# Even and odd outputs from channel sums: a new channel transform in the Fourier layer of a two-layer encoder

## The chip, the cores and the metric

The kernel runs on one core of one Trainium2 chip. The core has five engines, each with its own instruction queue that is worked off in order: PE (matmuls and transposes), DVE, ACT, POOL, and SP, which here only starts transfers. The metric is the device time of one execution in microseconds, the median of several runs; lower is better. One execution was also recorded by the hardware profiler, and all rows shown come from that recording.

## The reference

An encoder trunk of two layers runs on a prompt of 2048 positions and a sample of 512, with 1024 channels. Layer 0 is windowed attention. Layer 1, where the change lies, is a Fourier layer:

```python
def fourier_layer(x, g, w_gate, w_out):
    b, s, d = x.shape
    h = rmsnorm(x, g)
    hg = h.astype(jnp.float32).reshape(b, s, N_FGROUPS, FGROUP_CH)     # 4 groups of 256 channels
    f = jnp.fft.fftn(hg, axes=(1, 3), norm="ortho").real
    f = f.reshape(b, s, d).astype(x.dtype)
    gate = h @ w_gate
    return x + (f * jax.nn.silu(gate)) @ w_out
```

A final RMSNorm follows. The transform over a group's 256 channels is a product with a fixed 256x256 table of cosines and sines; the transform over positions comes later, out of its results.

## The kernel before

**Numbers.** [...] `matmul3` forms a product as higher x higher, higher x lower and lower x higher: three matmuls.

**The stage that matters.** The 20 tiles of 128 positions are worked off as ten `Pair`s. `gates(pr, hooks)` forms the gate of one pair as a two-by-two Strassen product in the order of its accumulators W, Z and X: W with B11, Z with T1 (on S1), W with T2 (on S2), Z with B22 (on S4), W with T3 (on S3), W with N4, and four short pieces of X between them; each is 12 matmuls of 512 columns, X is four times 3. Between these products the hooks prepare the next pair, `nx`:

- `norms` normalises its two tiles x[1] and x[0]; `turn` transposes one 512-channel half on PE into a PSUM bank and makes both parts of it (tile `tT`, ACT and DVE);
- `sums` forms F1, F2, F3 and F4, sums and differences of the transposed halves of the two tiles, in the tiles `s1` and `s4`; `parts` makes the two parts of each (tiles `S1` to `S4`, ACT and DVE);
- `z` is the channel transform: 24 matmuls of 256 columns for a tile, 12 for each of its halves `z..._0` and `z..._1`, on the parts of the transposes and the table `chan_sb`; ACT copies each half out of PSUM;
- `silu` turns a finished quarter of the gate (`c`, `c12` or W) into a tile `gt` (ACT tanh, DVE product), and POOL starts its store;
- after every second pair `combine` does a radix-4 step over the four z tiles of a group (six DVE additions of 1024 columns).

**What sets the order.** A scheduler puts the instructions into the five queues from the order of the text, the dependences and the free buffers; afterwards each queue is fixed. Buffers come from pools by tag. Two tags matter here: `x`, with four buffers of which one holds `chan_sb` throughout the stage, so that the tiles x[1], x[0], `c`, `s1` and `s4` of successive pairs share three; and `bank`, five PSUM banks for the transposes and z.

The buffers of the tag `x` are handed on like this before: `s1` of the next pair takes the buffer of that pair's x[1], which is free once its eight transposes have run.

The names of tiles carry numbers: `trb12_0` is a transpose of tile 12, `S1_3` the parts of F1 of pair 3, which is made of the tiles 12 and 8 and prepared inside the gates of pair 2 (`W2`, `X2`, `c2`).

Of the kernel before, what the change touches and what calls it, by code (L numbers as in the profile page):

```python
# [19 lines left out]
P = 128  # L20
# [11 lines left out]
HALVES = ((1, 0), (1, 1), (0, 0), (0, 1))  # L32
# [11 lines left out]
def encoder(  # L44
# [97 lines left out]
    def attention_phase():  # L142

        with ExitStack() as es:
# [484 lines left out]
            def gate_sums(k):  # L629
# [3 lines left out]
                def load():  # L633
                    for r in (k, k + 4):
# [69 lines left out]
            def quarters(place, k):  # L704

                t = ready["B", k] = place([P, 2, 512], F32, f"w32B_{k}")
                for half, r in enumerate((k, k + 4)):
                    after(SP.dma_start(t[:, half], w_gate[half, r // 2, :, (r % 2) * 512 : (r % 2) * 512 + 512]), last_exp[0])

            def ahead():  # L710

                def transform():
                    t = ready["chan"] = xtile([P, 2, 2, 256], F32R, "chan_sb")
                    after(POOL.dma_start(t, chan), last_exp[0])
# [17 lines left out]
                steps = dict(zip((42, 45, 48, 52), quarter + [transform]))  # L732
# [128 lines left out]
    def fourier_phase(tail):  # L861
        with ExitStack() as es:
# [55 lines left out]

            class Pair:
                def __init__(self, n, ts):  # L920
                    self.n, self.ts, self.x, self.ps, self.A, self.F, self.S = n, ts, [None, None], {}, {}, {}, {}
                    self.zs = [None, None]
# [11 lines left out]
                def turn(self, i, hf):  # L934
# [3 lines left out]
                    for k in range(4):  # L938
                        c0 = (hf * 4 + k) * P
                        PE.transpose(ps[:, k * P : (k + 1) * P], self.x[i][:, c0 : c0 + P], ident)  # L940
                    t = main.tile([P, 2, 512], F32R, align_bytes=LINE, tag="hT", bufs=8, name=f"tT{name}")
                    ACT.copy(t[:, 0], ps)
                    DVE.tensor_tensor(t[:, 1], ps, f32(t[:, 0]), ALU.subtract)
                    self.ps[i, hf], self.A[i, hf] = ps, (t[:, 0], t[:, 1])
# [16 lines left out]
                def parts(self, i):  # L961
                    self.S[i] = split(left([P, 2, 512], F32R, f"S{i}_{self.n}"), self.F[i])

                def z(self, i, hf):

                    t = self.ts[i]
                    if hf == 0:
                        self.zs[i] = zt(f"z{t}")
                    ps = bank(f"z{t}_{hf}")
                    a = self.A[i, hf]  # L970
                    for gg in range(2):
                        for kk in range(2):
                            ks = slice((gg * 2 + kk) * P, (gg * 2 + kk + 1) * P)
# [129 lines left out]
            def turns1(pr):  # L1103
                pr.turn(1, 0)
                pr.turn(1, 1)
                pr.sums(1)

            def turns2(pr):
# [5 lines left out]
                pr.parts(2)  # L1114

# [28 lines left out]
            for i, hf in HALVES:  # L1144
                pr.z(i, hf)
            for k in range(4):
                build(k)
            for n, pr in enumerate(pairs[:-1]):
                nx = pairs[n + 1]
                for i in range(2):  # L1150
# [4 lines left out]
                    5: [lambda: nx.z(1, 0), lambda: nx.z(1, 1)],  # L1155
                    6: [lambda: nx.z(0, 0), lambda: nx.z(0, 1), lambda: combine(nx)],
# [504 lines left out]
```

## Time and profile before

| | |
|---|---|
| median of three runs | 1620.09 us (1619.69 to 1620.53) |
| the profiled execution: its time / its span | 1622.4 us / 1620.6 us |
| busy: PE, DVE, ACT, POOL | 99%, 69%, 54%, 27% of the span |
| granted PE clock, mean | 0.995 |
| Fourier stage with z (first to last z matmul) | 1084.8 to 1330.9 us |
| one pair, from one W with B11 to the next | 26.63 us (1144.59 to 1171.22) |

The span is what the profiler saw between the first and the last instruction; the time has some start and end around it. A row of the timeline gives the start, the length of a run of like instructions, the engine, the line and the operation, and in brackets how long the engine had been idle and what ended that. A row of the groups gives the busy time and the mean length of one instruction in ns. PE's ends are modelled: consecutive matmuls overlap, so the step from one to the next is read from the starts of two rows, not from their lengths.

### The profile page before, as it was taken

How to read it: one execution, taken by the hardware profiler on the slowest of the kernel's cores; microseconds unless marked ns; L12 is line 12 of the kernel's file. 1: busy time of each engine (PE TensorE's matmuls, PEld its weight loads, DVE VectorE, ACT ScalarE, POOL GpSimd, SP SyncE). 2: the span in 40 equal slices, each digit the busy share in tenths (PEclk: the TensorE clock that was granted, in tenths of full speed). 3: DMA queues.
4: the chain of work that ended last, by engine and by line, in shares of the span. 5: the costliest groups of instructions: out<-in, count | busy, mean ns of one | idle time of the engine just before them, and what ended most of it. 6: DMA issues, size and time to landing. Idle time of an engine off the chain costs nothing.

```text
span 1620.6 us, 27520 instructions
## 1 busy us (share of the span) xinstructions
PE 1598.9 (99%) x9835; PEld 1334.6 (82%) x9835; DVE 1116.6 (69%) x2799; ACT 870.2 (54%) x2043; POOL 431.1 (27%) x605
## 2 busy tenths in 40 slices
PE   9999999999999999999999999999999999999998
PEld 7777888888888888978788888888888887888886
DVE  6788665777547776367754577668576767988696
ACT  6687644676237674157752476546545554343252
POOL 2456551421403414024222242211112111100010
PEclk9999999999999999999999999999999999999999
DMA  7487696656765567655659566666456469455952
GB/s 300 157 314 272 227 351 218 227 215 211 287 220 197 214 237 259 225 205 214 242 166 326 203 219 228 236 217 248 170 208 241 172 220 407 153 195 195 348 201 91
DMA packets 100644, 374.16 MB, mean 231 GB/s; under 512 B 12139, under 2 KB 22379, under 8 KB 83100
## 3 DMA queue, kind: packets, MB, share of 16 engines
q1 hardware_dynamic: 81708, 297.91, 51.8%
q0 software_dynamic: 16464, 70.30, 11.1%
q10 hardware_dynamic: 2336, 4.20, 0.7%
q8 instruction: 78, 1.28, 0.3%
q14 instruction: 58, 0.48, 0.1%
HBM read 281.10 MB, written 91.26 MB: 230 GB/s over the span
## 4 chain that ended last, share of the span: by engine, by line
PE 87%; DMA 5%; DVE 4%; ACT 2%; issue 1%; POOL 1%; SPq 0%; POOLq 0%; DVEq 0%; ACTq 0%
PE qp L95 13%; PE gp L95 12%; PE op L95 8%; PE spt L95 8%; PE W L95 6%; PE spt L441 6%; PE av L525 6%; PE fo L95 5%; PE z L95 4%; PE vp L95 4%; PE Z L95 3%; PE pt L499 3%; PE Wo L95 2%; PE X L95 2%; PE trb L940 1%; DMA xs<-in_x_dram 1%
## 5 line engine op out<-in xcount | busy, mean ns | idle before, releaser
L95 PE MATMUL qp<-h,wq 128*128 128x512 f32 x960 | 239.9, 399 | 0.2 <-DVE pts L508 0.2
L95 PE MATMUL gp<-h,wg 128*128 128x512 f32 x960 | 237.7, 396 | 0.0
L460 DVE CUSTOM_DVE_ANT_0 S<-spt,b 128x385 f32<-128x385 f32 (+1 forms) x320 | 156.9, 527 | 115.6 <-PE spt L441 115.2
L507 ACT CAST pts<-pt 128x384 fp32r<-128x384 f32 (+1 forms) x320 | 123.8, 472 | 185.6 <-PE pt L499 185.4
L95 PEld LDWEIGHTS qp<-h,wq 128*128 128x128 f32 x960 | 176.6, 190 | 42.6 <-issue 5.2
L95 PEld LDWEIGHTS gp<-h,wg 128*128 128x128 f32 x960 | 175.2, 188 | 43.5 <-issue 9.7
L468 ACT ACTIVATE S<-S 128x385 f32<-128x385 f32 (+1 forms) x320 | 190.1, 605 | 35.6 <-DVE S L460 35.1
L508 DVE TENSOR_TENSOR pts<-pt,pts 128x384 fp32r<-128x384 f32 (+1 forms) x320 | 147.3, 522 | 25.7 <-ACT pts L507 24.7
L549 POOL TENSOR_TENSOR uT<-o,uT 128x256 fp32r<-128x256 f32 x75 | 55.5, 740 | 358.9 <-ACT uT L548 358.9
L95 PE MATMUL op<-wo,uT 128*128 128x512 f32 x600 | 140.4, 391 | 0.0
L95 PE MATMUL fo<-wo,tTu 128*128 128x512 f32 x576 | 140.3, 395 | 0.0
L441 PE MATMUL spt<-kwin,qab 64*128 64x384 f32 (+1 forms) x960 | 132.6, 358 | 5.7 <-DVE S L460 5.6
L95 PEld LDWEIGHTS op<-wo,uT 128*128 128x128 f32 x600 | 111.9, 188 | 23.9 <-issue 0.7
L95 PEld LDWEIGHTS fo<-wo,tTu 128*128 128x128 f32 x576 | 106.8, 190 | 20.5
L525 PEld LDWEIGHTS av<-pts,v 128*128 128x128 f32 x576 | 101.4, 188 | 19.0 <-DVE pts L508 0.4
L441 PEld LDWEIGHTS spt<-kwin,qab 64*128 64x128 f32 x960 | 85.1, 185 | 37.5 <-issue 27.5
L525 PE MATMUL av<-pts,v 128*128 128x512 f32 (+1 forms) x576 | 115.9, 341 | 0.0
L95 PE MATMUL spt<-wo,uT 128*128 128x512 f32 x360 | 86.7, 392 | 0.0
L480 DVE TENSOR_SCALAR S<-S 128x384 f32<-128x384 f32 (+1 forms) x192 | 79.2, 413 | 5.3
L543 DVE TENSOR_TENSOR o<-av,t 64x256 f32<-64x256 f32 x150 | 62.6, 417 | 26.4 <-ACT t L534 25.0
L95 PEld LDWEIGHTS spt<-wo,uT 128*128 128x128 f32 x360 | 66.5, 188 | 13.7
L499 PEld LDWEIGHTS pt<-ident,S 64*128 64x128 f32 x1792 | 68.8, 138 | 6.2 <-issue 2.3
(304 smaller groups left out, 2937.5 us busy)
## 6 DMA issues: line engine op xcount, KB each, us to landing
wo<-wsd SPq DMA_DIRECT2D x32, 1024.0 KB, 5.2
wq<-wsd SPq DMA_DIRECT2D x31, 1024.0 KB, 7.4
wg<-wsd SPq DMA_DIRECT2D x31, 1024.0 KB, 4.9
x<-x1d SPq DMA_DIRECT2D x40, 512.0 KB, 3.6
b<-b21d SPq DMA_DIRECT2D x40, 512.0 KB, 5.1
b<-rowd SPq DMA_DIRECT2D x40, 384.0 KB, 4.3
xs<-in_x_dram SPq DMA_DIRECT2D x23, 512.0 KB, 6.5
s2d<-gt POOLq DMA_DIRECT2D x40, 256.0 KB, 3.4
```

The source lines that it names most:

```text
L95: pe(PE.matmul(out, a[i], b[j], start=start and i + j == 0, stop=stop and i == 1, skip_group_check=more))
L441: pe(PE.matmul(banks[j][:, 2 + k0 * P : 2 + k1 * P], res["q"][rows, qp, b * P : (b + 1) * P], kwin[g][rows, kp, b * P + k0 * P : b * P + k ...
L460: seq(DVE, DVE.tensor_tensor_reduce(out=s[:, e0:e1], in0=ps[:, 1 + e0 : 1 + e1], in1=st["bias"][:, j, 386 - e1 : 386 - e0][:, ::-1], scale ...
L468: last_exp[0] = seq(ACT, ACT.activation(s[:, e0:e1], s[:, e0:e1], AF.Exp, bias=s[:, 386:387], scale=-1.0, accum_out=s[:, 387:388]))
L480: seq(DVE, DVE.tensor_scalar(s[:, ks], s[:, ks], den, None, ALU.mult))
L499: pe(PE.transpose(ps[h][:, kb, j, :], ss[j][rows, 1 + kb * P : 1 + (kb + 1) * P], ident[rows, rows]))
L507: seq(ACT, ACT.copy(hi, ps[:, k0:k1]))
L508: seq(DVE, DVE.tensor_tensor(lo, ps[:, k0:k1], f32(hi), ALU.subtract))
L525: pe(PE.matmul(to, v, pt, start=n == part == 0, stop=part == 1 and n in (1, len(todo) - 1), skip_group_check=n > 1,))
L543: seq(DVE, DVE.tensor_tensor(o[64 * j : 64 * j + 64], ps[0:64, :, j], t2[:, :, j], ALU.add))
L549: low = eng.tensor_tensor(lo, o, f32(hi), ALU.subtract)
L940: PE.transpose(ps[:, k * P : (k + 1) * P], self.x[i][:, c0 : c0 + P], ident)
```

## The change

The channel transform is split by the parity of the output. For one group, the even outputs are a product of the sum of its two channel halves with a 128x128 table, the odd ones of the difference. `turn` therefore transposes, for each hf, the four groups' halves hf instead of four neighbouring blocks, and the gate's weights are paired to match (rows 2k and 2k+1 in place of k and k+4). What z multiplies is now:

- tile x[1]: even from F1 (which the gate's Strassen sums have anyway, `S1`), odd from the new `mb`, F1 minus twice the second half;
- tile x[0]: even from the new `ma`, odd from a new `mb`.

`mix` forms these f32 sums in place, in the x tiles themselves. `low` makes the parts: the higher one by ACT, the lower one by POOL in two pieces of 256 columns. It serves `ma`, `mb` and, in place of DVE, all four `parts`. The table's 256 columns hold its higher and its lower part side by side; so z takes 4 matmuls of 256 columns for a group (16 for a tile, 24 before), in a PSUM bank of its own, and the two 128-column results of each product are added on the way out: ACT copies one, DVE adds the other, into every second column. The transform's tile of `turn(1, 0)` is no longer made. The table is loaded raw into a free attention tile, and four ACT copies sort it.

```diff
             def ahead():
                 def transform():
+                    t = ready["table"] = ap.tile([P, 640], F32, tag="invb", name="chan32")[:, :512]
+                    after(POOL.dma_start(t, chan[:, 0].rearrange("p a c -> p (a c)")), last_exp[0])
+                def even_odd():
                     t = ready["chan"] = xtile([P, 2, 2, 256], F32R, "chan_sb")
-                    after(POOL.dma_start(t, chan), last_exp[0])
+                    src = ready["table"].rearrange("p (a n o) -> p o a n", a=2, o=2)
+                    for low in range(2):
+                        for odd in range(2):
+                            dst = t[:, low, odd].rearrange("p (a n) -> p a n", a=2)
+                            seq(ACT, ACT.activation(dst, src[:, odd], AF.Copy, scale=0.5 if low else 1.0))
...
                     for k in range(4):
-                        c0 = (hf * 4 + k) * P
+                        c0 = (k * 2 + hf) * P
                         PE.transpose(ps[:, k * P : (k + 1) * P], self.x[i][:, c0 : c0 + P], ident)
-                    t = main.tile([P, 2, 512], F32R, align_bytes=LINE, tag="hT", bufs=8, name=f"tT{name}")
-                    ACT.copy(t[:, 0], ps)
-                    DVE.tensor_tensor(t[:, 1], ps, f32(t[:, 0]), ALU.subtract)
-                    self.ps[i, hf], self.A[i, hf] = ps, (t[:, 0], t[:, 1])
+                    self.ps[i, hf] = ps
+                    if (i, hf) != (1, 0):
+                        t = htile([P, 2, 512], F32R, f"tT{name}")
+                        ACT.copy(t[:, 0], ps)
+                        DVE.tensor_tensor(t[:, 1], ps, f32(t[:, 0]), ALU.subtract)
+                        self.A[i, hf] = t[:, 0], t[:, 1]
+                def low(self, t, src):
+                    ACT.copy(t[:, 0], src)
+                    for j in range(2):
+                        cs = slice(j * 256, j * 256 + 256)
+                        POOL.tensor_tensor(t[:, 1, cs], src[:, cs], f32(t[:, 0, cs]), ALU.subtract)
+                    return t[:, 0], t[:, 1]
+                def mix(self, i):
+                    x, t = self.x[i].rearrange("p (o n) -> p o n", o=2), self.ts[i]
+                    if i == 0:
+                        ACT.copy(x[:, 0], self.ps[0, 0])
+                        DVE.tensor_tensor(x[:, 0], x[:, 0], self.ps[0, 1], ALU.add)
+                        self.M[0, 0] = self.low(htile([P, 2, 512], F32R, f"ma{t}"), x[:, 0])
+                    both = x[:, 0] if i == 0 else self.F[1]
+                    DVE.scalar_tensor_tensor(x[:, 1], self.ps[i, 1], -2.0, both, ALU.mult, ALU.add)
+                    self.M[i, 1] = self.low(htile([P, 2, 512], F32R, f"mb{t}"), x[:, 1])
...
                 def parts(self, i):
-                    self.S[i] = split(left([P, 2, 512], F32R, f"S{i}_{self.n}"), self.F[i])
-                def z(self, i, hf):
+                    self.S[i] = self.low(left([P, 2, 512], F32R, f"S{i}_{self.n}"), self.F[i])
+                    if i == 1:
+                        self.M[1, 0] = self.S[1]
+                def z(self, i):
                     t = self.ts[i]
-                    ...
-                            matmul3(
-                                ps[:, gg * 256 : gg * 256 + 256], (a[0][:, ks], a[1][:, ks]),
-                                (ch[:, kk, 0], ch[:, kk, 1]), kk == 0, kk == 1,
-                            )
-                    ACT.activation(
-                        self.zs[i][:, hf * 512 : hf * 512 + 512], ps, AF.Copy, scale=1.0 if t >= SEQ // P else 0.5
-                    )
+                    self.zs[i] = zt(f"z{t}")
+                    for g in range(4):
+                        ps = bank(f"z{t}_{g}")
+                        gs = slice(g * P, (g + 1) * P)
+                        for odd in range(2):
+                            m = self.M[i, odd]
+                            for part in range(2):
+                                PE.matmul(
+                                    ps[:, odd * 256 : odd * 256 + 256], m[part][:, gs], ch[:, t < SEQ // P, odd],
+                                    start=part == 0, stop=part == 1,
+                                )
+                        v = ps.rearrange("p (o a n) -> p a o n", o=2, a=2)
+                        out = self.zs[i][:, g * 256 : g * 256 + 256].rearrange("p (n o) -> p o n", o=2)
+                        ACT.copy(out, v[:, 1])
+                        DVE.tensor_tensor(out, out, v[:, 0], ALU.add)
...
             def turns1(pr):
                 pr.turn(1, 0)
                 pr.turn(1, 1)
                 pr.sums(1)
+                pr.mix(1)
             def turns2(pr):
...
                 pr.parts(2)
+                pr.mix(0)
```

The order of the queues changes with it. On ACT, in the gates of pair 2 where pair 3 is prepared, the rows before are these; `s1_3 <- trb12_0` starts F1, and the three rows `gt0_1`, `gt4_1`, `gt0_0` are the tanh of the gate's finished quarters:

```order
L952 COPY s1_3_13551<-trb12_0_13535 128x512
L883 CAST S1_3_13577<-s1_3_13551 128x512
L1037 COPY c12_2_13566<-W2_13500 128x512
L942 CAST tTb8_0_13573<-trb8_0_13568 128x512
L942 CAST tTb8_1_13585<-trb8_1_13580 128x512
L952 COPY s4_3_13588<-trb12_0_13535 128x512
L883 CAST S2_3_13590<-s1_3_13551 128x512
L883 CAST S4_3_13615<-s4_3_13588 128x512
L1011 ACTIVATE gt0_1_13611<-c12_2_13566 128x512
```

Now the copy that starts F1 stands behind all three, and the buffer that it fills is that of `c2`, which the third one and the DVE product behind it are the last to read:

```order
L1048 ACTIVATE gt0_1_13682<-c12_2_13624 128x512
L1048 ACTIVATE gt4_1_13708<-c2_13559 128x512
L1048 ACTIVATE gt0_0_13724<-c2_13559 128x512
L985 COPY s1_3_13604<-trb12_0_13591 128x512
L1048 ACTIVATE gt4_0_13769<-W2_13556 128x512
L962 CAST S1_3_13635<-s1_3_13604 128x512
L962 CAST mb12_13608<-x1_12_13538 128x512
L956 CAST tTb8_0_13631<-trb8_0_13626 128x512
L956 CAST tTb8_1_13644<-trb8_1_13639 128x512
L985 COPY s4_3_13647<-trb12_0_13591 128x512
```

The preparation of pair 3 on ACT has moved from before the gate's tanh rows to behind them.

On PE, from the last piece of X of pair 2 on, the rows before are:

```order
L95 MATMUL X2_13502<-b21_11_13596,tTb0_1_13338 128x512 x3
L95 MATMUL z12_0_13656<-chan_sb_12241,tTb12_0_13540 128x256 x12
L95 MATMUL z12_1_13670<-chan_sb_12241,tTb12_1_13548 128x256 x12
L95 MATMUL W2_13500<-wN4_0_12944,tTb4_1_13301 128x512 x3
L95 MATMUL W2_13500<-wN4_1_12953,tTb4_1_13301 128x512 x3
L95 MATMUL W2_13500<-wN4_2_12962,tTb4_1_13301 128x512 x3
L95 MATMUL W2_13500<-wN4_3_12971,tTb4_1_13301 128x512 x3
L95 MATMUL z8_0_13701<-chan_sb_12241,tTb8_0_13573 128x256 x12
L95 MATMUL z8_1_13715<-chan_sb_12241,tTb8_1_13585 128x256 x12
```

Now N4 follows the last piece of X at once, eight z matmuls of tile 12 (on `S1_3` and `mb12`) come behind it, and the rest stands among the first products of pair 3's gate (`W3`, `X3`, `Z3`). From the last of those eight on:

```order
L1010 MATMUL z12_1_13736<-chan_sb_12352,mb12_13608 128x256
L94 MATMUL W3_13831<-wB11_0_12757,tTb8_0_13631 128x512 x2
L94 MATMUL X3_13833<-b21_12_13693,tTb8_1_13644 128x512 x2
L1010 MATMUL z12_2_13743<-chan_sb_12352,S1_3_13635 128x256 x2
L1010 MATMUL z12_2_13743<-chan_sb_12352,mb12_13608 128x256 x2
L94 MATMUL W3_13831<-wB11_0_12757,tTb8_0_13631 128x512
L94 MATMUL W3_13831<-wB11_1_12775,tTb8_0_13631 128x512 x3
L94 MATMUL W3_13831<-wB11_2_12795,tTb8_0_13631 128x512 x3
L94 MATMUL W3_13831<-wB11_3_12737,tTb8_0_13631 128x512 x3
L94 MATMUL X3_13833<-b21_12_13693,tTb8_1_13644 128x512
L94 MATMUL Z3_13832<-wT1_0_12643,S1_3_13635 128x512
L1010 MATMUL z12_3_13750<-chan_sb_12352,S1_3_13635 128x256 x2
```

Behind these come two more z matmuls on `mb12`, one of Z3, and the sixteen of tile 8, on `ma8` and `mb8`, with one of Z3 among them; then the nine left of Z3 with T1. So the z of tile 12 has moved behind N4, and that of tile 8 into the next gate's product with T1.

On POOL only the stores of `gt` and the normalisation's powers stood in this stretch; now the lower parts stand in this order, two pieces each:

```order
L965 TENSOR_TENSOR S1_3_13635<-s1_3_13604,S1_3_13635 128x256 x2
L965 TENSOR_TENSOR mb12_13608<-x1_12_13538,mb12_13608 128x256 x2
L1052 DMA s2d0_82<-gt4_0_13769 128x512
L965 TENSOR_TENSOR S2_3_13649<-s1_3_13604,S2_3_13649 128x256 x2
L965 TENSOR_TENSOR S4_3_13686<-s4_3_13647,S4_3_13686 128x256 x2
L965 TENSOR_TENSOR ma8_13655<-x1_8_13547,ma8_13655 128x256 x2
L965 TENSOR_TENSOR S3_3_13714<-s4_3_13647,S3_3_13714 128x256 x2
L965 TENSOR_TENSOR mb8_13660<-x1_8_13547,mb8_13660 128x256 x2
```

Fourteen pieces a pair have come to POOL's queue, and `mb8`, which z of tile 8 needs, is the last.

More of the change, by code (lines that the diff above doesn't have):

```diff
@@ L31 @@
 LINE = 512
-HALVES = ((1, 0), (1, 1), (0, 0), (0, 1))
 LATE = (8, 9)
@@ L731, in ahead @@
                         lambda: sums(3), lambda: quarters(htile, 3)]
-                steps = dict(zip((42, 45, 48, 52), quarter + [transform]))
+                steps = dict(zip((42, 45, 48, 52, 56), quarter + [transform, even_odd]))
                 steps.update(zip(range(57, 65), mine))
@@ L1143, in fourier_phase @@
             more()
-            for i, hf in HALVES:
-                pr.z(i, hf)
+            for i in (1, 0):
+                pr.z(i)
             for k in range(4):
```

16 lines of the change are left out of this document (5 added, 11 removed).

## Prediction

> **What bounds the kernel now.** I read the page's engine shares first, then one pair of the gate stage by windows.
>
> ```profile
> span 1620.6 us, 27520 instructions
> PE 1598.9 (99%) x9835; PEld 1334.6 (82%) x9835; DVE 1116.6 (69%) x2799; ACT 870.2 (54%) x2043; POOL 431.1 (27%) x605
> 1144.59:1171.22 26.63, 26.63 (x150) 23.18 (x149) 14.71 (x23) 12.51 (x23) 3.33 (x6) 1.00 0.33 118
> 1171.22:1197.90 26.68, 26.68 (x151) 23.23 (x150) 21.37 (x30) 14.71 (x28) 5.51 (x10) 1.00 0.74 270
> ```
>
> PE is busy in the whole of both pairs, 26.65 us each (columns: length, then busy time of PE, weight loads, DVE, ACT, POOL, clock). So matmuls taken away are worth their time, and a wait put on PE costs all of its own. The timeline of one pair gives the steps and shows what now runs beside what.
>
> ```profile
> 1150.75 1.03 PE L940 MATMUL trb<-ident,x 128*128 128x128 f32 x8
> 1151.54 2.98 PE L95 MATMUL W<-wT,S 128*128 128x512 f32 x12
> 1152.78 0.59 ACT L952 COPY s<-trb 128x512 f32<-128x512 f32 x1 [0.27 <-DVE tTb L943]
> ...
> 1159.33 2.88 PE L95 MATMUL W<-wT,S 128*128 128x512 f32 x12
> ...
> 1162.05 0.84 PE L95 MATMUL X<-b,tTb 128*128 128x512 f32 x3
> ...
> 1162.25 0.69 DVE L1046 TENSOR_TENSOR c<-c,W 128x512 f32<-128x512 f32 x1 [0.83 <-PE W L95]
> ...
> 1162.73 3.04 PE L95 MATMUL z<-chan_sb,tTb 128*128 128x256 f32 x24
> 1162.93 0.69 DVE L1050 TENSOR_TENSOR c<-c,X 128x512 f32<-128x512 f32 x1
> ...
> 1165.60 2.91 PE L95 MATMUL W<-wN,tTb 128*128 128x512 f32 x12
> ```
>
> From start to start: a 512-column matmul 0.227 us (2.72 for twelve), a z matmul 0.120 (2.87 for 24), eight transposes 0.79. An engine takes over about 0.04 us after a record ends (X ends at 1162.89, DVE starts at 1162.93). F1's copy ran at 1152.78, ten us ahead of z: preparation was early, which is why z never waited.
>
> **The saving.** 24 matmuls become 16 for a tile: 20 x 8 x 0.120 = 19.1 us, 1.9 for a pair. Alone it gives 1601.
>
> **What is added on the way to z.** By the order, F1's copy now stands on ACT behind the tanh of the quarter that needs W with T3 and the last X. From there on a chain of single instructions leads to z, and their lengths are these groups' means.
>
> ```profile
> L952 ACT COPY s<-trb 128x512 f32<-128x512 f32 x20 | 12.1, 603 | 13.3 <-DVE tTb L943 13.3
> L883 ACT CAST S<-s 128x512 fp32r<-128x512 f32 x40 | 25.0, 627 | 19.1 <-DVE s L959 13.2 <-DVE S L884 4.6 <-PE W L95 1.0
> L1011 ACT ACTIVATE gt<-c 128x512 f32<-128x512 f32 x28 | 17.2, 627 | 9.5 <-DVE c L1041 8.5 <-DVE c L1046 0.6 <-DVE c L1050 0.4
> L1012 DVE SCALAR_TENSOR_TENSOR gt<-gt,c 128x512 f32<-128x512 f32 x28 | 18.9, 685 | 2.0 <-ACT gt L1011 1.6
> L959 DVE TENSOR_TENSOR s<-s,trb 128x512 f32<-128x512 f32 x20 | 13.6, 681 | 0.5
> L548 ACT CAST uT<-o 128x256 fp32r<-128x256 f32 x75 | 29.7, 396 | 0.0
> L1220 ACT COPY asp<-Ap 128x256 f32<-128x256 f32 x18 | 6.7, 375 | 23.0 <-PE Ap L95 13.5 <-DVE gp L1191 9.2
> L508 DVE TENSOR_TENSOR pts<-pt,pts 128x256 fp32r<-128x256 f32 x64 | 23.9, 415 | 0.6 <-ACT pts L507 0.6
> L549 POOL TENSOR_TENSOR uT<-o,uT 128x256 fp32r<-128x256 f32 x75 | 55.5, 740 | 358.9 <-ACT uT L548 358.9
> ...
> 734.54 1.43 POOL L627 TENSOR_TENSOR e<-w32e,e 128x256 fp32r<-128x256 f32 x2 [0.38 <-ACT e L683]
> ...
> L1015 POOL DMA_DIRECT2D s2d<-gt x40 | 22.2, 555 | 163.3 <-DVE gt L1012 158.3 <-issue 4.8
> ```
>
> A piece of a lower part takes POOL 0.74 us, and 0.70 from start to start (two in 1.43). I walk pair 3 through pair 2's gates, clock zero at the start of W with T3. PE: X at 2.72 (ends 3.56), N4 at 3.40, free at 6.12. DVE adds W 2.92 to 3.60 and X to 4.28; ACT's second tanh 4.32 to 4.95; DVE's product to 5.68; only then F1's copy, 5.72 to 6.32; DVE's add to 7.04 and `mb12` in f32 to 7.72; ACT casts S1 to 7.71, `mb12` to 8.39. POOL starts S1's pieces at 7.8 and 8.5, those of `mb12` at 9.2 (done 9.94) and 9.9 (10.64). PE's eight z matmuls of tile 12, the last two of them on the lower `mb12`, are through at 10.22 instead of 7.08: **first wait, 3.1**. The next bank is given back by the copy to `s4`, which fills the buffer of x[1] and so waits for POOL too (10.68 to 11.28): 0.2.
>
> The second wait comes from POOL's queue. After `gt`'s store (0.56, to 11.2) S2 needs its cast, which on ACT stands behind the `s4` copy and two z copies of 0.37: 12.65. S2's pieces start at 12.7 and 13.4; S4's cast is done at 14.25, and from then on POOL is never out of work: S4 14.3, ma8 15.7, S3 17.1, mb8 18.5 (first piece done 19.24, second 19.94). PE meanwhile, at 11.32, has 0.48 + 2.27 + 0.45 + 0.48 + 0.23 of z and products and reaches tile 8 at 15.23; it waits 1.1 for the lower `ma8` (16.44), works 0.7, and waits 2.1 for the lower `mb8` (19.24): **second wait, 3.2**. Eleven z matmuls and nine of Z with T1 end at 22.64.
>
> Queued behind: `c` of the next gate takes x[0]'s buffer, so its copy on ACT waits for `mb8` (19.94), and four z copies and the next Square stand behind it.
>
> ```profile
> L909 ACT ACTIVATE jkb<-x 128x1024 bf16<-128x1024 f32 x18 | 19.0, 1057 | 17.3 <-DMA x<-x1d 17.2
> L909 ACT ACTIVATION_READ_ACCUMULATOR jkb<-x 128x1 f32 x18 | 3.4, 187 | 0.0
> L932 DVE SCALAR_TENSOR_TENSOR x<-x,invb,g1b 128x1024 f32<-128x1024 f32 x18 | 23.1, 1284 | 14.6 <-POOL invb L89 14.6
> L89 POOL TENSOR_TENSOR invb<-invb,mhalf 128x1 f32<-128x1 f32 x20 | 11.6, 580 | 31.6 <-DVE invb L88 31.5
> L1071 DVE TENSOR_TENSOR z<-z,z 128x1024 f32<-128x1024 f32 x15 | 18.4, 1224 | 0.5
> x<-x1d SPq DMA_DIRECT2D x40, 512.0 KB, 3.6
> ```
>
> Copy to 20.57, z copies to 22.05, Square and its read (0.2) to 23.3, a small DVE step, the power (0.58), the scaling (1.28): x is ready at 25.5, and its transposes are due at 22.64 + 1.13: **third wait, 1.75**, in the pairs where they stand five matmuls into T2. In the others they stand later, but two 1.22 us radix-4 additions get between on DVE: two waits of some 0.55. SP's loads of x go out when POOL has finished S2 (14.14) and S3 (18.5) and land 3.6 later, in time for the Squares. POOL's power and stores stand behind `mb8`, done by then; they cost nothing while POOL is free at 19.94.
>
> Nine transitions: five of 3.1 + 0.2 + 3.2 + 1.75 = 8.25, four of 7.6: 71.7 us. In the first, F1's copy stands behind W's tanh as well: 1.1 more.
>
> **The start.** Pair 0 has no gate to hide its preparation.
>
> ```profile
> 1083.17 1.91 PE L940 MATMUL trb<-ident,x 128*128 128x128 f32 x16
> ...
> 1098.02 2.98 PE L95 MATMUL W<-wT,S 128*128 128x512 f32 x12
> ```
>
> After the sixteen transposes the same links bring the lower `mb17` at 1089.9, so that twelve z matmuls end at 1090.1 instead of 1086.5: 3.6. Then S2's cast at 1091.6 and nine pieces bring the lower `mb16` at 1098.0, with 0.4 and 1.9 of waits: 5.9 in all. Ends: 0 if the first products were to cover it, 5.9; I take 5.9, since none but 17 of them stand between.
>
> **Costed at nothing.** Weights paired otherwise: same tiles and pieces. The table's four ACT copies in the last attention chunk: 1.6 at most by a 256-column ACT cast of 0.4, 0 if PE's queue there covers them; 0, since the chunk's projections have work. The tile dropped for `turn(1, 0)` takes a 0.6 cast and a 0.68 subtraction off ACT and DVE, the four lower parts 2.7 off DVE, and eight z additions of 0.42 put 3.3 on; the walk holds them where they count. Writing every second column has no row; ACT and DVE might take from the same up to twice as long, 0 to 1.5 on the S2 cast's way; I take the same, by the 256-column rows.
>
> **The clock.** A short idle lowers it here:
>
> ```profile
> 44.97 1.05 PE L441 MATMUL spt<-kwin,qab 64*128 64x384 f32 x5 [2.02 <-DVE S L460]
> 42.00:45.00 3.00, 0.98 (x11) 0.56 (x9) 1.81 (x5) 1.59 (x3) 1.58 (x4) 1.00 0.83 339
> ...
> 46.00:47.00 1.00, 1.00 (x4) 0.81 (x4) 0.96 (x6) 0.70 (x4) 0.70 (x2) 0.50 0.00 0
> 47.00:48.00 1.00, 1.00 (x4) 0.81 (x3) 0.96 (x5) 1.00 (x4) 0.09 (x1) 0.50 0.44 188
> 48.00:49.00 1.00, 1.00 (x5) 0.76 (x4) 0.88 (x5) 0.06 (x1) 0.00 (x0) 0.63 1.06 451
> ```
>
> After 2.02 us of idle the clock is 0.50 for some 3.4 us: 1.7 us of matmuls lost. The first wait's drop falls where PE would wait for `ma8` and `mb8` anyway, 0. The second's falls on T1 and T2; in five pairs the third wait swallows it, in four it costs 1.7 less half a microsecond, 1.2: 5. [...]
>
> **The sum.** -19.1 + 71.7 + 1.1 + 5.9 + 5 = +64.6. On the profiled execution (1622.4, span 1620.6) 1687; on the median, 2.3 below it, 1620.1 + 64.6 = **1685**.
>
> **Rivals.** *The waits are covered* (faster, 1601): z of tile 8 would have to get its lower parts by 12.8, where PE would be without waits. That needs POOL's fourteen pieces in about 0.2 us each instead of 0.70; no POOL row is near it. 0.05. *Only the first wait holds*: S2's cast and POOL's tail come earlier than I have them, the second wait goes, and a third of one remains: 9 x 4.3 - 19.1 + 3.6 = +23, 1643. Against it: POOL has 14 x 0.70 = 9.8 us of pieces from 7.8 on, and a store. 0.08. *The clock pays more*: the third wait lowers it again, 1.7 more in all nine: +15, 1700; for it speaks the row at 44.97, against it that 1.75 is shorter than 2.02. 0.25. *The change doesn't do what it says*, PE taking longer for a z matmul whose banks alternate: at most 0.04 x 320 = 13 more; the same 256-column form ran at 0.120. 0.02.
>
> My forecast has 0.60. With POOL never out of work (thirteen pieces and the store, 17.5 for `mb8`) and no third wait, T1 ends at 20.9, and with 8.4 of T2, transposes, B22 and X a transition takes 29.3, 2.6 more than now: 24 in nine, and 3.7 at the start, 1648 in all; that is the low end. The high end, 1708, takes in the clock case and 1.5 us of slow writes in five pairs. A change within 0.2% (3 us) can't be told from none: faster 0.05, same 0.01, slower 0.94.
>
> **What would show it.** z matmuls 320 instead of 480 at about 0.12 us step; PE idle before z some 30 us for each of the two POOL-fed waits, ended by POOL `mb`, `ma` and S; PE at about 95%; POOL near 530 us; a pair about 32.5 us instead of 26.65; the clock below 1.00 between 1085 and 1390. I am wrong if z starts without waiting, or if POOL's lower parts take much less than 0.7 us.

## The result, and the profile after

The changed kernel takes 1683.09 us (median of four runs, 1681.25 to 1686.24), the kernel before 1619.89 us beside it (1619.68 to 1620.53): a ratio of 1.038, interval [1.036, 1.040]. It is slower by 63 us; 1685 was forecast.

The page of the changed kernel, its first lines (busy time, share of the span, instructions):

```profile
span 1680.5 us, 27588 instructions
...
PE 1613.8 (96%) x9675; PEld 1326.3 (79%) x9675; DVE 1136.0 (68%) x2859; ACT 892.6 (53%) x2117; POOL 535.2 (32%) x745
```

PE has 160 matmuls fewer and is busy for longer. At half clock 17.7 us are lost (added up under "The half clock" below), less than the 19.1 that the missing matmuls took; what else lengthens the busy time is not separated, and the ends of PE's records are modelled. Three successive pairs by windows (length, then busy time of PE, weight loads, DVE, ACT and POOL, the clock):

```profile
1154.18:1186.64 32.46, 27.88 (x132) 22.47 (x132) 16.76 (x30) 15.69 (x33) 13.07 (x20) 0.95 0.35 130
1186.64:1219.75 33.11, 28.21 (x132) 22.50 (x133) 23.78 (x36) 15.99 (x33) 16.96 (x24) 0.95 0.52 191
1219.75:1252.33 32.58, 27.61 (x132) 22.33 (x133) 16.76 (x30) 15.69 (x33) 13.09 (x20) 0.95 0.35 129
```

A pair took 26.65 before, PE busy throughout; now 32.5 to 33.1, with PE idle for 4.6 to 5 of it. The waits of PE show for whom (total, times, longest):

```profile
PE z L1010 <- POOL mb L965: 17.4, 21, 1.8
PE z L1010 <- ACT S L962: 14.6, 10, 3.2
...
PE trb L952 <- DVE invb L87: 4.2, 4, 1.3
PE trb L952 <- DVE x L944: 3.7, 7, 0.6
PE z L1010 <- POOL S L965: 3.6, 11, 0.4
```

z, which never waited before, waits for S and for `mb`, and the next pair's transposes wait for x and for its scale `invb`. The timeline of one pair on PE shows where:

```profile
1182.43 3.02 PE L94 MATMUL W<-wN,tTb 128*128 128x512 f32 x12
1186.64 0.50 PE L1010 MATMUL z<-chan_sb,S 128*128 128x256 f32 x2 [1.19 <-ACT S L962]
1187.51 0.51 PE L1010 MATMUL z<-chan_sb,S 128*128 128x256 f32 x2 [0.36 <-POOL S L965]
1187.85 0.40 PE L1010 MATMUL z<-chan_sb,mb 128*128 128x256 f32 x2
1188.89 0.50 PE L1010 MATMUL z<-chan_sb,mb 128*128 128x256 f32 x2 [0.65 <-POOL mb L965]
1189.23 0.63 PE L94 MATMUL W<-wB,tTb 128*128 128x512 f32 x2
...
1195.64 0.28 PE L1010 MATMUL z<-chan_sb,ma 128*128 128x256 f32 x1
1197.68 1.01 PE L1010 MATMUL z<-chan_sb,mb 128*128 128x256 f32 x3 [1.76 <-POOL mb L965]
...
1209.82 1.07 PE L952 MATMUL trb<-ident,x 128*128 128x128 f32 x8 [0.38 <-DVE x L944]
```

N4 began at 1182.43 and has 12 x 0.227 = 2.72 of work, to 1185.15. The eight z matmuls (0.96) are through at 1189.23, when W of the next gate starts: 4.08 less 0.96 is 3.1 us of wait. Then the lower `mb` of the other tile (a lower part is a tile less its cast copy, the higher part) is missing for 1.9 (1195.76 to 1197.68).

The stretch from the first transpose to the last z matmul carries the whole loss: 1083.17 to 1330.9 before, 1081.86 to 1394.8 after, 65 us longer.

### The profile page after: what moved, and what is told of

Its sections match the earlier page's. It is cut to its first block, busy times and chain, and to the rows that moved or that the text cites. A ratio compares the mean times of both kernels' runs of the same rounds, so it can differ in the third digit from the quotient of the medians.

```text
span 1680.5 us, 27588 instructions
## 1 busy us (share of the span) xinstructions
PE 1613.8 (96%) x9675; PEld 1326.3 (79%) x9675; DVE 1136.0 (68%) x2859; ACT 892.6 (53%) x2117; POOL 535.2 (32%) x745
## 5 line engine op out<-in xcount | busy, mean ns | idle before, releaser
L507 DVE TENSOR_TENSOR pts<-pt,pts 128x384 fp32r<-128x384 f32 (+1 forms) x320 | 147.3, 522 | 25.3 <-ACT pts L506 24.2
L524 PEld LDWEIGHTS av<-pts,v 128*128 128x128 f32 x576 | 101.4, 188 | 19.1 <-DVE pts L507 0.4
```

The source lines that it names most:

```text
L507: seq(DVE, DVE.tensor_tensor(lo, ps[:, k0:k1], f32(hi), ALU.subtract))
L524: pe(PE.matmul(to, v, pt, start=n == part == 0, stop=part == 1 and n in (1, len(todo) - 1), skip_group_check=n > 1,))
```

## The experiments

One measure goes through all of them: the mean length of a pair, from the start of N4 in pair 2's gate to its start in pair 8's, six pairs. An even number is taken because in some of these kernels N4 stands in every second pair behind the next gate's W with B11, and long and short pairs alternate. In the timeline of the changed kernel these two rows are:

```profile
1182.43 3.02 PE L94 MATMUL W<-wN,tTb 128*128 128x512 f32 x12
...
1378.44 0.50 PE L94 MATMUL W<-wN,tTb 128*128 128x512 f32 x1
```

(1378.44 - 1182.43) / 6 = 32.67. The other kernels, read the same way:

| kernel | median us | ratio to before | N4 of pair 2, of pair 8 | a pair |
|---|---|---|---|---|
| before | 1619.9 to 1622.1 | | 1165.60, 1325.36 | 26.63 |
| changed | 1683.09 | 1.038 [1.036, 1.040] | 1182.43, 1378.44 | 32.67 |
| before, 16 matmuls a tile | 1604.64 | 0.990 [0.986, 0.993] | 1161.65, 1312.69 | 25.17 |
| s1 elsewhere | 1647.89 | 1.016 [1.013, 1.018] | 1177.79, 1351.56 | 28.96 |
| mixed sums elsewhere | 1628.04 | 1.004 [1.003, 1.005] | 1174.16, 1331.43 | 26.21 |
| lower parts by DVE | 1651.96 | 1.019 [1.016, 1.021] | 1173.78, 1348.41 | 29.11 |
| both of these | 1618.98 | 0.999 [0.998, 1.000] | 1167.37, 1319.09 | 25.29 |
| waits filled | 1683.88 | 1.038 [1.036, 1.040] | 1185.49, 1379.90 | 32.40 |
| before, S1 to S4 by POOL | 1640.34 | 1.011 [1.009, 1.014] | 1172.98, 1345.98 | 28.83 |
| the same, s1 and s4 elsewhere | 1629.17 | 1.004 [1.002, 1.005] | 1175.39, 1337.99 | 27.10 |
| mixed sums elsewhere, ma and mb by DVE | 1629.87 | 1.006 [1.004, 1.007] | 1167.53, 1330.55 | 27.17 |
| mixed sums elsewhere, S1 to S4 by DVE | 1624.91 | 1.001 [1.000, 1.003] | 1173.40, 1327.82 | 25.74 |
| mixed sums, s1 and s4 elsewhere | 1638.94 | 1.010 [1.009, 1.012] | 1178.95, 1339.55 | 26.77 |
| both, and an earlier start | 1621.93 | 1.001 [1.000, 1.002] | 1173.83, 1325.09 | 25.21 |

**The saving by itself.** The kernel before with the table's lower part left out of z, so that a tile has 16 matmuls; nothing else moves.

```diff
-                            matmul3(
-                                ps[:, gg * 256 : gg * 256 + 256], (a[0][:, ks], a[1][:, ks]),
-                                (ch[:, kk, 0], ch[:, kk, 1]), kk == 0, kk == 1,
-                            )
+                            for part in range(2):
+                                PE.matmul(
+                                    ps[:, gg * 256 : gg * 256 + 256], a[part][:, ks], ch[:, kk, 0],
+                                    start=kk + part == 0, stop=kk + part == 2,
+                                )
```

> The kernel before with the product of higher part and the table's lower part left out of z: 16 matmuls of 256 columns for a tile instead of 24, nothing else changed (the transform loses the table's lower part). It measures the saving by itself: 160 x 0.120 = 19 us if z matmuls are worth their time, 1601; if other engines bind as soon as PE has less to do, less than 19.

Measured: 1604.64 beside 1621.13, 16.5 us less. Pairs of 24.7, the full 1.9 less, alternate with pairs of 25.3 to 26.0, in which Z now waits for the product `gt` that frees its bank (0.3 to 0.9); and once, in the first pair, the transposes wait 1.9 for x:

```profile
PE trb L940 <- DVE x L932: 2.2, 2, 1.9
PE Z L95 <- DVE gt L1013: 1.9, 3, 0.9
```

So matmuls taken from PE are worth most of their time here (16.5 of 19.1 us), and the preparation had not quite the 1.9 us a pair to spare.

**Which part makes the waits: s1's buffer.** `s1` gets a buffer of the tag R (sixteen buffers, those of the z tiles and of X's blocks `b` among others), so that F1's copy need not wait for the buffer of `c`; its place on ACT is ahead of the tanh rows again.

```diff
                     if i in (1, 4):
-                        self.pair = xtile([P, 2, 512], F32, f"s{i}_{self.n}")
+                        self.pair = (right if i == 1 else xtile)([P, 2, 512], F32, f"s{i}_{self.n}")
```

> The changed kernel with one tile moved: s1 (F1 and F2) takes a buffer of the tag R instead of the tag x, so that it no longer waits for the gate's c. Theory A (the preparation starts late because mix keeps the x buffers and s1 gets that of c): F1's copy stands ahead of the gate's tanh again, some 8 us earlier in a pair, POOL's 14 pieces end before z, and nearly all waits before z go: 1601 plus about 4 us at the start, 1605. Rival B (POOL's lower parts are too slow wherever they start): the waits on POOL mb and ma stay, about 3 us a pair, and the time is 1630 or more.

Measured: 1647.89, 35 us less than the changed kernel, but far from 1605. The waits for `mb` fell from 17.4 to 3.5 and those for S from 14.6 to 2.3; a new one came, PE's Z for a `gt` of the gate before, 13.2 in all. The timeline of that kernel over PE, POOL, ACT, DVE and SP's queue shows its chain, once every second pair:

```profile
1176.50 1.44 POOL L965 TENSOR_TENSOR mb<-x,mb 128x256 fp32r<-128x256 f32 x2
1177.79 2.91 PE L94 MATMUL W<-wN,tTb 128*128 128x512 f32 x12
1177.96 2.31 SPq L939 DMA_DIRECT2D x<-x1d  x2
...
1185.43 1.06 ACT L918 ACTIVATE jkb<-x 128x1024 bf16<-128x1024 f32 x1 [1.32 <-DMA x<-x1d]
...
1186.49 0.58 ACT L1048 ACTIVATE gt<-W 128x512 f32<-128x512 f32 x1
...
1188.70 0.68 DVE L1049 SCALAR_TENSOR_TENSOR gt<-gt,W 128x512 f32<-128x512 f32 x1
...
1189.44 5.49 PE L94 MATMUL Z<-wT,S 128*128 128x512 f32 x12 [3.39 <-DVE gt L1049]
```

The sums are still mixed in the x tiles, so a load of the next x goes out only when POOL has read the last of them (1177.94, load at 1177.96). The Squares wait for the loads, and behind them on ACT stands the tanh of the gate's last quarter: W was complete by 1180.7, its tanh ran at 1186.49. The DVE product behind that tanh is the last reader of W's bank, which Z needs. Neither theory had this wait: A was wrong on the time, B on what is waited for.

**The mixed sums in tiles of their own.**

```diff
                 def mix(self, i):
-                    x, t = self.x[i].rearrange("p (o n) -> p o n", o=2), self.ts[i]
+                    x, t = zt(f"mx{self.ts[i]}").rearrange("p (o n) -> p o n", o=2), self.ts[i]
```

> The changed kernel with mix's f32 sums in a tile of the tag R instead of in place in the x tile, so that x is free after its transposes as before; lower parts stay on POOL. Theory A: as with s1 moved, about 1605, if the b21 loads that share the tag R are not late. Rival B: 1630 or more, as POOL is unchanged.

Measured: 1628.04, 55 of the 63 us gone, with POOL still forming all lower parts. x[1] is free after its transposes again, `s1` takes its buffer, and F1's copy is back ahead of the tanh rows (in one pair of its timeline at 1161.87, the first tanh at 1169.82). The time lies between the two theories, nearer to B's 1630; a pair takes 26.21, 1.0 above the kernel with 16 matmuls.

**The lower parts on DVE**, in one piece of 512 columns, the sums still in the x tiles.

```diff
                     ACT.copy(t[:, 0], src)
-                    for j in range(2):
-                        cs = slice(j * 256, j * 256 + 256)
-                        POOL.tensor_tensor(t[:, 1, cs], src[:, cs], f32(t[:, 0, cs]), ALU.subtract)
+                    DVE.tensor_tensor(t[:, 1], src, f32(t[:, 0]), ALU.subtract)
```

> The changed kernel with low's subtraction on DVE in one piece instead of POOL in two; buffers and the late start stay. Theory A: the second wait (3.2 us a pair) goes, the first shrinks from 3.1 to about 2.1, the start loses 2 to 3 us of waits, the late start itself stays: 1683 less about 9 x 4 less 2, 1645. Rival B: without POOL the waits go altogether and the time is about 1605.

Measured: 1651.96; the pair is 3.6 us shorter than the changed one. The waits of PE in this kernel:

```profile
PE z L1008 <- ACT S L962: 15.5, 10, 3.3
PE W L94 <- DVE c L1081: 6.9, 5, 1.6
```

The POOL-fed wait is gone, the one for S, whose preparation still starts behind the tanh, is all there. Theory A, though the time is 7 us above its 1645: N4 now waits for the addition to `c` on DVE (6.9 in all), a wait that neither theory had.

**Both at once.** The two edits above together.

> The changed kernel with both suspects taken away: the mixed sums in tiles of their own and all lower parts on DVE, 0.68 us each. Theory A (the place of the sums and POOL's queue are the whole loss, and what the mixed sums in tiles of their own still lost, 1628, is POOL's queue at the start and in single waits): 1605 to 1616, faster than before. Rival B (DVE, with 4.8 us a pair more, then comes too late with the transposes' tiles and the quarter sums): 1625 or more, waits ended by DVE.

Measured: 1618.98, ratio 0.999 [0.998, 1.000]: the whole loss is gone, but no gain is shown. Its pairs take 25.29, 0.12 more than those of the kernel with 16 matmuls (25.17), so in the steady stage nearly all of that saving is there. Much of what is lost lies ahead of it: from the first transpose to N4 of pair 1 it takes 62.97 (1080.73 to 1143.70), the kernel before 55.80 (1083.17 to 1138.97). Of these 7.2 us 2.7 are only order, the next gate's W with B11, which stands ahead of N4 here; against that 40 z matmuls less have run, 4.8 us. What is lost there is idle time, 5.7 us of it on PE (before: 0.03), and some 1.7 of matmul time at half clock. The three longest of its six recorded waits there:

```profile
1084.46 1.31 PE L1008 MATMUL z<-chan_sb,S 128*128 128x256 f32 x4 [1.82 <-ACT S L962]
...
1141.39 0.48 PE L1008 MATMUL z<-chan_sb,S 128*128 128x256 f32 x2 [0.82 <-DVE mx L974]
...
1143.70 4.37 PE L94 MATMUL W<-wN,tTb 128*128 128x512 f32 x12 [1.59 <-DVE c L1081]
```

Five of the six, 3.6 us, end with DVE, which in this kernel is busy for 144.0 of the 155 us from 1155 to 1310 (before: 107.5). So A was right on the cause and 3 us too low in its range; B's wait is there too, at a smaller price.

Taken alone, the place of the sums is worth 55 us and POOL 31; together they are worth 64, not 86. That with the sums elsewhere the preparation starts early enough to hide most of POOL's work is the likely reason.

**POOL alone, in the kernel before.** Only `parts` is changed: POOL forms the lower parts of S1 to S4.

```diff
-                    self.S[i] = split(left([P, 2, 512], F32R, f"S{i}_{self.n}"), self.F[i])
+                    t = left([P, 2, 512], F32R, f"S{i}_{self.n}")
+                    ACT.copy(t[:, 0], self.F[i])
+                    for j in range(2):
+                        cs = slice(j * 256, j * 256 + 256)
+                        POOL.tensor_tensor(t[:, 1, cs], self.F[i][:, cs], f32(t[:, 0, cs]), ALU.subtract)
+                    self.S[i] = t[:, 0], t[:, 1]
```

> The kernel before with one part of the change alone: POOL, not DVE, forms the lower parts of S1 to S4, in two pieces of 256 columns each, eight pieces or 5.6 us a pair. Theory A (POOL's 0.70 us a piece hurts only where the preparation starts late; here F1's copy starts ten us ahead of z, and the parts are wanted by the next pair's gate): 1617 to 1626, no difference. Rival B (the lower parts on POOL are late by themselves, whatever the order): above 1632, with PE waiting for POOL S.

Measured: 1640.34, 19 us slower. Theory A is wrong; B has the size, but PE does not wait for POOL. It waits for `gt` (12.3 in all), by the same chain as above, with `s4` in the place of the x tile. Its timeline over SP's queue, POOL, ACT, DVE and PE:

```profile
1136.54 9.48 SPq L927 DMA_DIRECT2D x<-x1d  x2
...
1143.79 1.88 POOL L966 TENSOR_TENSOR S<-s,S 128x256 fp32r<-128x256 f32 x2 [4.45 <-ACT S L963]
...
1149.67 1.06 ACT L909 ACTIVATE jkb<-x 128x1024 bf16<-128x1024 f32 x1 [4.01 <-DMA x<-x1d]
...
1150.73 0.58 ACT L1016 ACTIVATE gt<-W 128x512 f32<-128x512 f32 x1
...
1152.96 0.68 DVE L1017 SCALAR_TENSOR_TENSOR gt<-gt,W 128x512 f32<-128x512 f32 x1
...
1153.69 4.58 PE L95 MATMUL Z<-wT,S 128*128 128x512 f32 x12 [4.06 <-DVE gt L1017]
```

POOL ends the last piece on `s4` at 1145.67; the second of the two loads is issued by 1146.02, lands for the Square at 1149.67, and tanh, product and Z follow.

**The link tested: s1 and s4 in R**, otherwise as the last one.

```diff
-                        self.pair = xtile([P, 2, 512], F32, f"s{i}_{self.n}")
+                        self.pair = right([P, 2, 512], F32, f"s{i}_{self.n}")
```

> The run of the kernel before with S1 to S4's lower parts on POOL, but the tiles s1 and s4, which POOL reads, take buffers of the tag R instead of x. There PE waited 12.3 us for Z's bank, which the product on W frees; its tanh stood on ACT behind the Square of a tile x whose load had been late. Theory A (POOL's late pieces hold the x buffer of s4, so the next load goes out late; the buffer is the link): 1617 to 1627, no difference from before, and no wait of Z for gt over 1 us. Rival B (the parts themselves are late, or ACT's order is worse whatever the buffers): 1635 to 1645 as there.

Measured: 1629.17, ratio 1.004 [1.002, 1.005]; no wait of Z for `gt` over 0.31 is left, so the buffer is the link. The time is 2 us outside A's range. X now waits 4.2 us, in four waits, for the blocks `b`, whose tag `s1` and `s4` share, and the first transposes wait 1.6 for an addition on DVE that belongs to the layer before; which of them makes the 2 us is not shown.

**Half of the lower parts on POOL, and more tiles out of x.** On the kernel with the mixed sums elsewhere (1628.04), first `ma` and `mb` go to DVE and S1 to S4 stay on POOL, then the other way round (`split` is False for `ma` and `mb`, then for the four `parts`).

```diff
-                def low(self, t, src):
+                def low(self, t, src, split=True):
                     ACT.copy(t[:, 0], src)
+                    if not split:
+                        DVE.tensor_tensor(t[:, 1], src, f32(t[:, 0]), ALU.subtract)
+                        return t[:, 0], t[:, 1]
```

> As the run with the mixed sums in tiles of their own, but the lower parts of ma and mb go to DVE and only those of S1 to S4 stay on POOL (eight pieces a pair instead of fourteen). Theory A (in that run POOL's queue still cost the start and part of each pair): 1612 to 1622. Rival B (what was left there is not POOL's): 1625 to 1632, as there.

Measured: 1629.87, ratio 1.006 [1.004, 1.007]: no gain from taking six of fourteen pieces off POOL. The time is B's, but its reason does not hold, for with the other eight off POOL as well it is 1618.98. The waits of PE that are left here end with DVE, to which the six came: z waits 5.5 us for the mixed sums and N4 4.6 for the addition to `c`.

> The changed kernel with the mixed sums in tiles of their own and S1 to S4's lower parts on DVE; only those of ma and mb stay on POOL, six pieces a pair. Theory A (POOL hurts through the tiles s1 and s4, whose x buffers the next loads wait for; ma and mb no longer hold such a buffer, so their pieces on POOL are covered): 1608 to 1617, as good as with all lower parts on DVE or better. Rival B (any lower part on POOL costs): 1623 to 1632.

Measured: 1624.91, ratio 1.001 [1.000, 1.003], pairs of 25.74. The pairs are 0.45 longer than with DVE alone, and 1.4 shorter than with the other eight pieces on POOL (27.17), so those on `s1` and `s4` are the dearer ones, as A has it; but the time is in B's range. From the first transpose to N4 of pair 1 it takes 64.94, 2 us longer than with DVE alone.

Then, with all lower parts on POOL, `s1` and `s4` out of x as well (the edit of the run before these two):

> The changed kernel with POOL forming all lower parts as it does, but neither the mixed sums nor s1 and s4 in buffers of the tag x: nothing that POOL reads holds a buffer that a load of x waits for. Theory A (the buffers are the whole mechanism, POOL's 0.70 us a piece only its size): 1608 to 1620. Rival B (POOL's fourteen pieces are late for z by themselves): 1628 or more, waits ended by POOL mb and ma.

Measured: 1638.94, ratio 1.010 [1.009, 1.012], worse by 11 us. Two of the new waits of PE:

```profile
PE z L1010 <- DVE z L1017: 6.6, 4, 2.1
...
PE X L94 <- DMA b<-b21d: 2.8, 2, 1.4
```

A is wrong, and B's wait for POOL (`mb`, 3.6) is only one of several. `b`, which shares the tag R, comes late again, but only twice. Most of the 11 us lies ahead: from the first transpose to N4 of pair 1 it takes 71.95 (1082.94 to 1154.89), with the mixed sums alone elsewhere 62.94 (1086.61 to 1149.55). Why the start is that much longer is not shown.

**The half clock.** In the changed kernel, 24 matmuls a pair are put where PE waits; the products overwrite them.

```diff
+                def fill(self, out, anchor):
+                    for _ in range(12):
+                        after(PE.matmul(out, wg["N4"][0][0][:, :P], ch[:, 1, 0], start=True, stop=True), anchor)
...
                             m = self.M[i, odd]
+                            if g == 0 and odd != i and anchor is not None:
+                                self.fill(ps[:, odd * 256 : odd * 256 + 256], anchor)
```

> The changed kernel with 24 matmuls of 256 columns a pair added, 216 in all, whose results are overwritten before use: twelve stand in the last stretch of N4, ahead of the first wait for S1 and mb of tile x[1], twelve ahead of the wait for the lower mb of tile x[0]. At 0.120 us each they are 25.9 us of PE work put where PE was idle. Theory A (the half clock after the waits, 17.7 us of matmul time by the windows of the changed kernel's profile, is paid in full): the waits are as before but the clock stays near 1.00, so the time falls in spite of the added work, to 1665 to 1673. Rival B (what the half clock costs is mostly swallowed by the next wait, as the forecast's 5 us had it): 1678 to 1686. Rival C (the waits do not shrink by what is filled in, because what PE waits for is itself made later): up to 1709.

Measured: 1683.88, as without them, though 25.9 us of work were added. The stage by one window, the changed kernel and this one (the clock is the third number from the end):

```profile
1085.00:1390.00 305.00, 260.08 (x1212) 207.13 (x1213) 188.48 (x303) 151.97 (x309) 138.42 (x204) 0.94 0.45 165
```

```profile
1085.00:1390.00 305.00, 274.09 (x1426) 222.90 (x1425) 185.68 (x301) 150.28 (x309) 133.80 (x203) 0.98 0.46 166
```

By windows of 1 us, busy time x (1 - clock) adds up to 17.7 us in the changed kernel from 1083 to 1390 and to 4.8 here, all of it in the first transitions. Its steady pairs take 32.40, 0.27 less than 32.67, with 2.9 us more matmuls in each. Behind both fillings of the pair looked at PE still waited for POOL (0.64 for `mb` at 1191.81 and 0.27 at 1201.15, by its timeline), so the filling itself took nothing from such a pair. So of the 12.9 us that came back from the half clock, an estimated 9 x 0.27 = 2.4 had cost time. Rival B; A is ruled out.

**A version with an earlier start.** The kernel with both edits, and for pair 0 alone the first half of x[0] transposed first, so that W with B11 covers the preparation.

```diff
             def turns2(pr):
-                pr.turn(0, 0)
+                if pr.n:
+                    pr.turn(0, 0)
...
             pr = pairs[0]
+            pr.turn(0, 0)
             turns1(pr)
```

> The run with the mixed sums in tiles of their own and all lower parts on DVE, and one thing more: for the first pair alone the transposes of tile x[0], first half, come first, so that the gate's first product, W with B11, runs while the parts of S1 and mb are made. In that run PE waited 1.82 us there, and its first pair ran 5.9 us longer than in the run of 16 matmuls without lower table. Theory A (the start is what is left between these two runs, and W with B11 covers most of it): 1613 to 1617, faster than before by over 0.2%. Rival B (the wait only moves, to Z or to the transposes of the next pair): 1617 to 1621, the same as before.

Measured: 1621.93, ratio 1.001 [1.000, 1.002]. Its pairs take 25.21, but the wait moved, and from the first transpose to N4 of pair 1 it takes 67.31 (1083.17 to 1150.48), 4.3 more than without this edit. PE waits in the first pair of this kernel's timeline:

```profile
1092.95 0.47 PE L1008 MATMUL z<-chan_sb,S 128*128 128x256 f32 x2 [2.02 <-DVE mx L974]
...
1112.71 0.51 PE L94 MATMUL W<-wT,S 128*128 128x512 f32 x1 [1.30 <-ACT wT L892]
```

z now waits for the mixed sum, and the product on T3 for its weights. Rival B. No version here that keeps the table's lower part beats the kernel before by more than its measurement tells.

## Why the prediction was right

- **The saving**, -19.1: 16.5 by the kernel that has it alone, since a wait at the start and one in every second pair take back part of it.
- **The first wait**, 3.1: 3.1 by the rows of the pair shown. Its cause, F1's copy behind the tanh because the mixed sums keep x's buffers, is shown: with `s1` elsewhere the waits for S and `mb` fell to 2.3 and 3.5 in all, with the sums elsewhere to 1.8 and 0.6. Its largest part, 1.19, ends with ACT's cast of S, and is the same 1.19 with the lower parts on DVE; so it comes of the late start, not of POOL.
- **The second wait**, 3.2 from POOL's queue: 1.9 for `mb` and, in the pair shown, 0.6 for `ma`. In the pairs beside it the wait for `mb` is 1.5 and 1.9, and the half clock after the first wait takes up the rest, as the walk had it: over the nine transitions these waits come to 12.7 us by the records, 1.4 each, and the matmul time lost at half clock to 16.0, 1.8 each. With the lower parts on DVE the pair is 3.6 shorter.
- **The third wait**, 1.75 or two of 0.55: too high. PE's recorded waits for `invb` are 4.2 in four (the longest 1.3), those for x 3.7 in seven (the longest 0.6): 7.9 together, where five of 1.75 and four of 1.1 make 13.2.
- **The transitions together**: the forecast makes a pair 33.0 or 32.35 (26.65 - 1.9 + 8.25 or 7.6); measured 32.67 in the mean. From the first N4 to the last, nine transitions, the changed kernel takes 297.9 (1112.56 to 1410.48), the kernel before 240.3 (1112.35 to 1352.67): 57.6 more, where 71.7 + 1.1 - 9 x 1.9 is 55.7, and 60.7 with the clock's 5. Six pieces of X, 1.4 us, are in the 57.6 only because they stand behind the first N4 now.
- **The first transition** was mis-sized: 37.42 against 26.62, 10.8 more, 9.4 without those pieces of X, where at most 8.25 + 1.1 - 1.9 = 7.45 was forecast. In it the clock was at half twice by windows of 1 us (1113 to 1115, 1123 to 1126), and z waited 3.24 for S, the longest of all.
- **The start**, 5.9: between the first transpose and N4 of pair 0 PE was idle for 4.2 us (before: 0.03), and 1.7 of matmul time were lost at half clock. Its first part, 3.6, came: W follows the first twelve z matmuls 7.0 us after the first transpose (1081.86 to 1088.87), 3.3 before (1083.17 to 1086.47). Of the 2.3 for the lower `ma` and `mb` only 0.3 came. In their place stand the half clock and 1.5 of waits of W for T3's weights and for `c`, which the walk did not have, so that this part fits in size by luck.

```profile
1088.87 1.06 PE L94 MATMUL W<-wB,tTb 128*128 128x512 f32 x2
...
1096.62 0.50 PE L1010 MATMUL z<-chan_sb,mb 128*128 128x256 f32 x2 [0.31 <-POOL mb L965]
```

- **The clock**, +5: an estimated 2.4. The rival that had it pay 15 more is out: by windows of 1 us the clock falls at most once in a steady pair, behind waits of z, and never behind a wait of the transposes; and most of what is lost at half clock would have been waited away. The rows behind it, PE's timeline of one pair and the window after:

```profile
1154.18 0.50 PE L1010 MATMUL z<-chan_sb,S 128*128 128x256 f32 x2 [1.19 <-ACT S L962]
1155.05 0.51 PE L1010 MATMUL z<-chan_sb,S 128*128 128x256 f32 x2 [0.36 <-POOL S L965]
...
1156.42 0.56 PE L1010 MATMUL z<-chan_sb,mb 128*128 128x256 f32 x2 [0.64 <-POOL mb L965]
1156.78 1.06 PE L94 MATMUL W<-wB,tTb 128*128 128x512 f32 x2
```

```profile
1157.00:1158.00 1.00, 1.00 (x3) 0.79 (x3) 0.79 (x2) 0.91 (x3) 0.58 (x2) 0.50 0.00 0
```

  Three gaps of at most 1.19 were followed by 0.50 here (1157 to 1160); in the pair shown above the same three were not (1.00 from 1186 to 1197; two products of W take 0.63 at 1189.23, where they take 1.06 at 1156.78), and the clock fell only behind the 1.76 (0.50 from 1198 to 1201). What decides whether a gap lowers the clock is not shown.
- **Costed at nothing**: the table's copies, rightly (the first transposes start at 1081.86, before at 1083.17). Writing every second column, ACT took 400 ns in the median, where its 256-column copies before had 375 in the mean, and DVE 416, where it had 415:

```profile
L1016 ACT COPY z<-z x80: 385/400/446, 1088.2 to 1395.1; 128x256 f32<-128x256 f32 x80
L1017 DVE TENSOR_TENSOR z<-z,z x80: 409/416/430, 1092.3 to 1395.6; 128x256 f32<-128x256 f32 x80
```

- **The signs**: PE's idle time before z was to be some 30 us for each of two waits fed by POOL. By the records it is 36.5 in all: 17.4 for `mb`, 14.6 for ACT's cast of S, 3.6 for POOL's part of S, 0.9 for `ma`. The other signs came: PE at 96%, POOL at 535 us, the pair at 32.67, the clock at 0.94.

The mechanism was right where it counts: the first two waits, with the half clock that takes up part of the second, are the large terms, and both causes are shown. That the sum came within 2 us is luck in part: the third wait and the clock were too high by about as much as the first transition and the saving were too favourable, and part of the start fits by other waits than those walked.

What stays open: why `ma` and `mb` on POOL alone still cost some 6 us against DVE (1624.91 and 1618.98, not timed side by side; the pairs, 0.45 longer, make up some 4 of them), and how the waits at the start of the kernel with both edits, most of which end with DVE, could be covered; putting W with B11 over the first one only moved them.

## What to carry to other kernels

When a tile is used in place for one more step, ask who waits for its buffer: here giving these sums tiles of their own, with the same arithmetic, brought back 55 of the 63 us. The loss came through a queue order that changed and loads that went out late. A slower engine on the preparation (POOL, 0.73 us for 256 columns, where DVE takes 0.68 for 512) cost most here where a buffer that a load needs hung on it: S1 to S4's lower parts on POOL alone cost 19.1 us with `s1` and `s4` in such buffers, 7.1 with them elsewhere. The wait then showed up far away, under another engine's name (Z for DVE's `gt`, 12.3). And where PE waits for a producer, matmuls at half clock (an estimated 2.4 of 12.9 us), or added ones (25.9 us for less than 1), cost little here, so a low clock in the rows is no proof of a loss. When pairs of work are compared between kernels, see that the same work stands ahead of both marks.

## What the hardware showed that was not expected

Filling PE's waits with 25.9 us of matmuls kept the clock near 1.00 in the steady pairs (0.98 instead of 0.94 over the stage) and changed the time by less than 1 us. The granted clock fell to 0.50 (1157 to 1160) behind gaps of which none was longer than 1.2 us in one pair, and stayed at 1.00 (1186 to 1197) behind the same gaps in the next.
